# A decoder block on one core: the first norm's squares taken from transposed blocks, the first unit's weight remainders by accumulating transfers, and the rotation tables beside the gated units

## The chip, the core and the metric

The kernel runs on 1 core of one Trainium2 chip. The time is device microseconds of one execution of the whole block, and what counts is the median of several runs. Three runs of the kernel before took 1307.81, 1310.59 and 1313.95 us.

## The reference

One layer of a decoder, 512 tokens of width 1024, all in float32. In order: half a gated feed-forward network (hidden width 2816), a mixer with two branches (a convolution over 31 tokens with a layer norm, and a dilated attention with rotary position codes), a second half network, a gated embedding of the layer, and a last norm.

```python
h = h + 0.5 * swiglu(rms_norm(h, g_ffn1), w_ffn1_gate, w_ffn1_up, w_ffn1_down)
u = rms_norm(h, g_mix)
z = u @ w_in                              # conv gates | q | k | v | merge gates
y_conv = conformer_conv(a_glu, ...)       # glu, 31 taps, layer norm, silu, @ w_conv_out
q, k = rotary(q, cos, sin), rotary(k, cos, sin)
y_attn = o.reshape(b, s, ATTN_OUT_W) @ w_attn_out
h = h + (g_a * y_conv + g_b * y_attn) @ w_mix_out
h = h + 0.5 * swiglu(rms_norm(h, g_ffn2), w_ffn2_gate, w_ffn2_up, w_ffn2_down)
h = h + sigmoid(rms_norm(h, g_ple) @ w_ple_gate) * (p @ w_ple_proj)
return rms_norm(h, g_final)
```

Here `swiglu(x)` is `(silu(x @ w_gate) * (x @ w_up)) @ w_down`, and `cos` and `sin` come from the tokens' positions.

## The kernel before, in words

**Precision.** TensorE multiplies in a shortened float32. So each operand is split into a high part `h` (ScalarE copies it to the short type) and a remainder `l`, and a product is three matmuls: high by high, high by low, low by high (`mm3`, L458). A weight tile of 128 x 1024 is a *slab*. Its remainder is made in one of two ways. In `split_one` (L392) ScalarE makes `h` and VectorE subtracts, `l = r - h`. In `early_one` and `remainder` (L369 to L390) ScalarE writes `-h` into `l`, and a transfer issued by POOL adds the raw slab `r` to it in memory; ScalarE copies twice and VectorE does nothing. `by_dma` (L256) says which slabs go the second way. Raw slabs `wr`, sums `s`, `wh` and `wl` share sixteen buffers.

**The order.** `slab_order` (L132) lists all slabs, and `slab` (L440) loads, sums and splits ahead of use by fixed counts. There is no scheduler: each engine gets its instructions in the order in which the code is run, and waits in order.

**A network** (`ffn`, L779). Gate and up columns come in eleven units. Unit 0 is computed plainly: `plain` runs over the eight 128-row pieces of the input in two halves, four slabs (`gq`), into banks `pg` and `pu`. Units 1 to 10 (`gate_up`, L901) and the down steps (`down`, L953, called `dn` 1 to 5) use seven products in place of eight: B11, B21, T2, T1, T3, B22, T4, on sums of input quarters (`forms`, `form_pair`) and of weight quarters (`sum_one`). A product of a unit is 24 matmuls, with its result in banks `pa`, `pe` or `pd`. Unit 0's result goes through a plain down step (`down_plain`, L975) late in the network, where it needs its own split `hidh`, `hidl` (`keep`, L784, L790 and L792). `PLAN` (L73) is the order: units 1, 2, 3, `dn` 1, and so on to units 8, 9, `dn` 4, unit 10, the plain step, `dn` 5.

**The norm's factor.** The input is used unnormalised, and the factor of each token, 1/rms, is multiplied in after the matmuls. `token` (L871) computes it: sums of squares, a root by VectorE (`rsqrt`, L558), and two diagonal matrices. `on_all` (L618) spreads it over all partitions by two matmuls into a tile `R`. `gated` (L816) then makes unit 0's result from `R` and the four banks `pg` and `pu`; `others` makes the parts for T3 and T4. In the first network the squares are eight ScalarE passes over the columns of `x` with seven VectorE additions, and eight small matmuls (`ss`, L593) in the middle of the second half. The block's rows are made by `row_block` (L1088): four transposes of `x` by TensorE into a bank `tp` and a ScalarE copy; eight of these, from a list `turns`, one behind each of the first eight products.

**The tables** (`tables`, L1036) are some 36 VectorE instructions on 128 x 512 and two sines on ScalarE, put into a queue `bg` when unit 2 of the first network begins. `background(n)` runs the next `n` entries of `bg`; the counts `TABLES`, `TABLES_P` and `TABLES_D` place them beside products of the first network.

**The convolution.** For each pair of channel tiles of the gated units (`glu`, L1159; c = 0 to 7), `conv_start` puts some 64 entries into `bg`, which VectorE works off beside the gated units, the attention and the merge gates: six beside each half of a gated unit from c = 1, and six beside each merge gate. When `bg` is empty, `half` and `side` (L1525 to L1534) run the steps of the layer norm, `lns`: mean, centring, root, spreading to `R`, eight products with `R` (L1496), eight Silus (L1500) and splits into `cvh`, `cvl` (L476, L477). What is left of them by the end of the attention projection (banks `pb`) is run there at once, ahead of the eight `co` units (banks `py`), which need all eight `cvh` and `cvl`.

Of the kernel before, what the change touches and what calls it, by code (L numbers as in the profile page):

```python
# [18 lines left out]
P = 128  # L19
S = 512  # L20
D = 1024
# [27 lines left out]
N_NORM = {"1": ((1, 2), (1, 7)), "2": ((0, 6), (1, 3))}  # L49
# [30 lines left out]
TABLES = {"T3": 1, "B22": 1}  # L80
TABLES_P = 1
TABLES_D = {"B21": 1, "T3": 1, "B22": 1}
# [71 lines left out]
def block_kernel(ctx: ExitStack, tc: tile.TileContext, a, out):  # L154
# [101 lines left out]
    def by_dma(key):  # L256
        return product(key) in BY_DMA or key[0] in POOLED + RAISED or key[0] == "gq" and key[2] > 0
# [254 lines left out]
    def begin(norm):  # L512
# [40 lines left out]
        for c in range(KD):  # L553
            norm.add(x[c])
# [11 lines left out]
    class Norm:  # L566
# [18 lines left out]
        def total(self, m, by=None):  # L585
# [5 lines left out]
            for b in range(NB):  # L591
                for i, t in enumerate(every):
                    PE.matmul(p[:, b:b + 1], by_class(t)[:, b] if by else t[:, b * P:(b + 1) * P], mean[:, 0:1], start=i == 0,  # L593
                              stop=i == len(every) - 1)
            V.tensor_scalar(m, p[:, :NB], EPS, None, op0=OP.add)

        def by_token(self, diag=True, *by):
            m, y, t = (small.tile([P, NB], F32, name=name(q), tag="nt" + q, bufs=2) for q in "myt")
            self.total(m, *by)
# [11 lines left out]
        def spread(self):  # L611
            p = bank("R")
# [5 lines left out]
        def on_all(self):  # L618
            p, R = self.spread(), T("R")
# [4 lines left out]
    class Rows(Norm):  # L624
# [6 lines left out]
        def add(self, b, x_):  # L631
            A.activation(T("sq"), h[b][:, x_ * S:(x_ + 1) * S], AF.Square, scale=D ** -0.5,
# [146 lines left out]
    def ffn(n, xs, u, norm, out_, soon_=None, last_=None):  # L779
# [45 lines left out]
        def forms():  # L825
# [24 lines left out]
            for c, t12 in enumerate(t12s):  # L850
# [4 lines left out]
                flush(2)  # L855

# [14 lines left out]
        def token():  # L871
            y = norm.by_token(True, *([True] if n == "1" else []))
# [28 lines left out]
        def gate_up(j):  # L901

            ps = {q: bank(q) for q in ("pa", "pe", "pd")}
            t = {}
# [5 lines left out]
            for q in PRODUCTS:  # L910
                wh, wl = slab((n, ("gu", j), q))
                p = ps[BANKS[q]]
                while any(q not in z for z in xn):
                    next_job()
                quarters_of(p, q, wh, wl, [z[q] for z in xn])
                if q in ("B11", "T2", "T1"):
# [30 lines left out]
                background(TABLES.get(q, 0))  # L947
                if turns:
                    turns.pop(0)()
# [834 lines left out]
```

## Time and profile before

| what | value |
|---|---|
| profiled execution, its own time | 1308.47 us |
| its span | 1306.7 us |
| TensorE busy | 1272.3 us, 97% |
| VectorE busy | 1070.6 us, 82% |
| ScalarE busy | 756.1 us, 58% |
| POOL busy (it issues transfers) | 219.9 us, 17% |
| transfers by POOL, share of the 16 DMA engines | 51.2% |
| transfers by SP and ScalarE, share | 20.8% |

In the profile PE is TensorE, DVE is VectorE, ACT is ScalarE, and L736 is line 736 of the kernel. A line of instructions gives start and duration in us, then line, operation, and output and input by the program's names, then the count; in brackets stands how long the engine had been idle before it, and what ended that. Matmuls overlap, so the time that one takes from its neighbours is the distance of two starts, not its duration. In a table by stretch each engine has its busy time and, in brackets, its instructions; behind POOL's stands the clock that TensorE was granted, as a share of full speed. A line of waits gives the total in us, how often, and the longest.

### The profile page before, as it was taken

How to read it: one execution, taken by the hardware profiler on the slowest of the kernel's cores; microseconds unless marked ns; L12 is line 12 of the kernel's file. 1: busy time of each engine (PE TensorE's matmuls, PEld its weight loads, DVE VectorE, ACT ScalarE, POOL GpSimd, SP SyncE). 2: the span in 40 equal slices, each digit the busy share in tenths (PEclk: the TensorE clock that was granted, in tenths of full speed). 3: DMA queues.
4: the chain of work that ended last, by engine and by line, in shares of the span. 5: the costliest groups of instructions: out<-in, count | busy, mean ns of one | idle time of the engine just before them, and what ended most of it. 6: DMA issues, size and time to landing. Idle time of an engine off the chain costs nothing.

```text
span 1306.7 us, 20040 instructions
## 1 busy us (share of the span) xinstructions
PE 1272.3 (97%) x7546; PEld 1128.7 (86%) x7546; DVE 1070.6 (82%) x1733; ACT 756.1 (58%) x1098; POOL 219.9 (17%) x284
## 2 busy tenths in 40 slices
PE   8799999999999999999999999999999999999997
PEld 7799989897788889898988888888898999998786
DVE  8679898989767987777788866698988888887975
ACT  7576656665653235656475545355676766665573
POOL 0011111111132223323232222100111111111000
PEclk9899999999899999999999999999999999999999
DMA  7367776867798889888787877755568687777531
GB/s 248 89 164 187 194 178 165 208 139 179 167 217 185 194 187 178 161 193 153 166 163 179 193 173 180 197 129 162 145 178 210 148 208 169 192 201 179 147 97 65
DMA packets 120265, 224.43 MB, mean 172 GB/s; under 512 B 19048, under 2 KB 63464, under 8 KB 120168
## 3 DMA queue, kind: packets, MB, share of 16 engines
q0 software_dynamic: 44416, 136.33, 51.2%
q1 hardware_dynamic: 75464, 86.56, 20.8%
q8 instruction: 59, 0.97, 0.3%
q14 instruction: 38, 0.31, 0.1%
q10 hardware_dynamic: 288, 0.26, 0.1%
HBM read 164.36 MB, written 2.13 MB: 127 GB/s over the span
## 4 chain that ended last, share of the span: by engine, by line
PE 78%; DVE 8%; DMA 5%; issue 3%; ACT 2%; DVEq 0%; SPq 0%; POOL 0%; POOLq 0%; ACTq 0%
PE pa L736 4%; PE pa L737 4%; PE pa L739 4%; PE pq L459 4%; PE pq L460 4%; PE pq L461 4%; PE pa L746 3%; DMA wl<-wr 3%; PE pg L459 3%; PE pa L747 3%; PE pg L461 3%; PE pa L751 3%; PE pg L460 3%; DMA wr<-in_w_ffn_down 2%; PE pd L739 2%
## 5 line engine op out<-in xcount | busy, mean ns | idle before, releaser
L374 POOL DMA_DIRECT2D wl<-wr x104 | 89.2, 858 | 671.5 <-ACT wl L372 515.6
L403 DVE TENSOR_TENSOR wl<-s,wh 128x1024 fp32r<-128x1024 f32 x96 | 117.3, 1222 | 56.2 <-ACT wh L402 55.6
L1136 DVE SCALAR_TENSOR_TENSOR acc<-glu,taps,acc 128x511 f32<-128x511 f32 (+14 forms) x240 | 161.6, 733 | 0.0
L737 PE MATMUL pa<-bl,wh 128*128 128x256 f32 x480 | 120.3, 287 | 8.0 <-DVE bl L834 7.9
L736 PE MATMUL pa<-bh,wh 128*128 128x256 f32 x480 | 120.0, 287 | 3.7 <-ACT p L918 3.7
L372 ACT ACTIVATE wl<-wr 128x1024 fp32r<-128x1024 f32 x104 | 109.0, 1048 | 18.1 <-PE pd L751 8.3
L402 ACT ACTIVATE wh<-s 128x1024 fp32r<-128x1024 f32 x96 | 100.5, 1051 | 28.0 <-PE pa L751 7.9
L386 ACT ACTIVATE wh<-wr 128x1024 fp32r<-128x1024 f32 x104 | 108.8, 1046 | 1.9 <-PE pd L751 1.0
L372 ACT ACTIVATE wl<-wh 128x1024 fp32r<-128x1024 f32 x76 | 79.4, 1050 | 51.3 <-DMA wh<-in_w_in 32.4
L737 PEld LDWEIGHTS pa<-bl,wh 128*128 128x128 f32 x480 | 93.5, 195 | 9.0 <-DVE bl L834 9.0
L736 PEld LDWEIGHTS pa<-bh,wh 128*128 128x128 f32 x480 | 93.5, 195 | 4.5 <-ACT p L918 4.5
L459 PE MATMUL pq<-xsh,wh 128*128 128x512 f32 x224 | 88.7, 396 | 0.0
L460 PE MATMUL pq<-xsl,wh 128*128 128x512 f32 x224 | 87.3, 390 | 0.0
L461 PE MATMUL pq<-xsh,wl 128*128 128x512 f32 x224 | 87.3, 390 | 0.0
L374 POOL DMA_DIRECT2D wl<-in_w_in x56 | 48.6, 868 | 220.9 <-ACT wl L372 210.2
L739 PE MATMUL pa<-bh,wl 128*128 128x256 f32 x480 | 68.2, 285 | 0.0
L459 PE MATMUL pg<-xsh,wh 128*128 128x512 f32 x160 | 64.0, 400 | 0.3 <-DVE xsh L487 0.3
L460 PE MATMUL pg<-xsl,wh 128*128 128x512 f32 x160 | 63.2, 395 | 0.7 <-DVE xsl L488 0.6
L461 PE MATMUL pg<-xsh,wl 128*128 128x512 f32 x160 | 62.9, 393 | 0.0
L739 PEld LDWEIGHTS pa<-bh,wl 128*128 128x128 f32 x480 | 62.7, 194 | 0.0
L762 DVE SCALAR_TENSOR_TENSOR gx<-pa,half,gx 128x512 f32<-128x512 f32 x80 | 56.3, 747 | 1.6 <-PE pa L751 1.6
L746 PE MATMUL pa<-wh,bh 128*128 128x512 f32 x136 | 53.9, 396 | 2.7 <-DVE gx L762 2.7
(352 smaller groups left out, 3802.4 us busy)
## 6 DMA issues: line engine op xcount, KB each, us to landing
wl<-wr POOLq DMA_DIRECT2D x104, 512.0 KB, 5.1
wh<-in_w_in POOLq DMA_DIRECT2D x56, 512.0 KB, 7.2
wl<-in_w_in POOLq DMA_DIRECT2D x56, 512.0 KB, 6.2
wr<-in_w_ffn_up SPq DMA_DIRECT2D x88, 256.0 KB, 4.9
wr<-in_w_ffn_down SPq DMA_DIRECT2D x44, 512.0 KB, 5.3
wr<-in_w_ffn_gate SPq DMA_DIRECT2D x86, 256.0 KB, 5.0
wh<-in_w_v POOLq DMA_DIRECT2D x16, 256.0 KB, 7.1
wl<-in_w_v POOLq DMA_DIRECT2D x16, 256.0 KB, 5.6
```

The lines of the kernel that those rows point to most:

```text
L372: A.activation(l.bitcast(F32R), h, AF.Copy, scale=-1.0)
L374: G.dma_start(to, src, accum_op=OP.add)
L386: A.activation(h, r, AF.Copy)
L402: A.activation(h, r, AF.Copy)
L403: V.tensor_sub(l, r, h.bitcast(F32))
L459: PE.matmul(ps, wh, xh, start=start, stop=False, skip_group_check=part)
L460: PE.matmul(ps, wh, xl, start=False, stop=False, skip_group_check=part)
L461: PE.matmul(ps, wl, xh, start=False, stop=stop, skip_group_check=part)
L736: PE.matmul(o, h[:, c], th, start=q in ("B11", "B21", "T1") and i == 0, stop=False, skip_group_check=True)
L737: PE.matmul(o, h[:, c], tl, start=False, stop=False, skip_group_check=True)
L739: PE.matmul(o, l[:, c], th, start=False, stop=i >= len(at) - 2, skip_group_check=True)
L1136: bg.append(lambda acc=acc, g=g, w=w, s=s: V.scalar_tensor_tensor(acc[:, s:], g[:, :S - s], w, acc[:, s:], op0=OP.mult, op1=OP.add))
```

## The change

Five things are changed together.

- *Squares.* The first network's sums of squares come from `row_block`: while a transposed block lies in its bank, ScalarE squares it with a sum along each row, and then copies it. All eight blocks now stand in the second half of unit 0, one at each k. `token` follows product B11 of unit 1, and `on_all`, `gated` and `others` follow B21.
- *Remainders.* The four products of unit 1 that VectorE split (T2, T1, T3, B22), in both networks, and the four `gq` slabs of the second network get their remainders by accumulating transfers.
- *Tables.* They are put into `bg` after the first network, ahead of the convolution's entries: ten run after the gated unit c = 0, the rest in the next free places.
- *Plain down step.* `hidh` and `hidl` are made from unit 9 on, a unit earlier, in both networks.
- *Smaller.* The banks of a unit are taken when first used, and in the second network `gated` comes ahead of `others`.

```diff
--- before.py
+++ after.py
...
-N_NORM = {"1": ((1, 2), (1, 7)), "2": ((0, 6), (1, 3))}
+N_NORM = ((0, 6), (1, 3))
...
-TABLES = {"T3": 1, "B22": 1}
-TABLES_P = 1
-TABLES_D = {"B21": 1, "T3": 1, "B22": 1}
...
-        return product(key) in BY_DMA or key[0] in POOLED + RAISED or key[0] == "gq" and key[2] > 0
+        return (product(key) in BY_DMA or key[0] in POOLED + RAISED or key[:2] == ("gq", "2")
+                or key[0] in ("1", "2") and key[1] == ("gu", EARLY))
...
-        for c in range(KD):
-            norm.add(x[c])
...
+        def spread(self, tag="ps"):
+            p = bank("R", tag)
...
+        def on_all(self, tag="ps"):
+            p, R = self.spread(tag), T("R")
...
+        def add(self, b, x_, src=None):
+            A.activation(T("sq"), h[b][:, x_ * S:(x_ + 1) * S] if src is None else src, AF.Square, scale=D ** -0.5,
                          accum_out=self.cols[:, x_ * NB + b:x_ * NB + b + 1])
 
...
                 flush(2)
+            flush(0)
...
             us_ = [lambda i=i: slab(("gq", n, 0, 2 * half + i)) for i in range(2)]
-            fs = {k: f for (at, k), f in zip(N_NORM[n], (token, lambda: R.append(norm.on_all()))) if at == half}
-            if soon_ and half == 0:
-                fs[2] = soon_
+            fs = {}
+            if n == "1" and half:
+                fs = {k: turns.pop(0) for k in range(KD)}
+            elif n == "2":
+                fs = {k: f for (at, k), f in zip(N_NORM, (token, lambda: R.append(norm.on_all()))) if at == half}
+                if half == 0:
+                    fs[2] = soon_
             done.append(plain(us_, fs))
             if half == (n == "1"):
                 others = forms()
             if n == "2":
                 work(10.9)
+        hooks = {}
         if n == "1":
+            while jobs:
+                next_job()
+
+            def spread(done=done, others=others):
+                R.append(norm.on_all("cv"))
+                gated(*done)
+                while jobs:
+                    next_job()
+                others()
+                done.clear()
+            hooks = {"B11": token, "B21": spread}
+        else:
             gated(*done)
             others()
             work(10.9)
-        else:
-            others()
-            gated(*done)
-            work(10.9)
         done = others = None
 
...
-            ps = {q: bank(q) for q in ("pa", "pe", "pd")}
-            t = {}
+            ps, t = {}, {}
...
+                if BANKS[q] not in ps:
+                    ps[BANKS[q]] = bank(BANKS[q])
                 p = ps[BANKS[q]]
                 while any(q not in z for z in xn):
                     next_job()
                 quarters_of(p, q, wh, wl, [z[q] for z in xn])
+                if q in hooks:
+                    hooks.pop(q)()
...
-                background(TABLES.get(q, 0))
-                if turns:
-                    turns.pop(0)()
...
-                if not last:
-                    background(TABLES_D.get(q, 0))
...
-                    background(2 * TABLES_P)
...
-                if key[1] == KF // 2 - 1:
+                if key[1] == KF // 2 - 2:
                     keep(0, early[0])
                     early[0] = None
-                if n == "1" and key[1] == 2:
-                    tables()
...
-    norm = Norm()
-    x, xs, u1 = begin(norm)
-    norm.flush()
+    norm = Rows()
+    x, xs, u1 = begin()
...
     def row_block(b, j):
 
         p = bank("tp", "cv")
         for i in range(KD // 2):
             PE.transpose(p[:, i * P:(i + 1) * P], by_class(x[4 * j + i])[:, b], ident)
+        norm.add(b, j, p)
         A.activation(h[b][:, j * S:(j + 1) * S], p, AF.Copy)
...
-    background(len(bg))
+    tables()
...
-        if c == 1:
+        if c == 0:
+            background(10)
             rc, rs = tabs["cos"], tabs["sin"]
-            V.tensor_mul(rc, rc, R[0])
-            V.tensor_mul(rs, rs, R[0])
+            for t in (rc, rs):
+                bg.append(lambda t=t: V.tensor_mul(t, t, R[0]))
         if c % 2:
             conv_start((c - 1, c), glus)
             glus = []
```

On TensorE, in the first network, these rows stood in the second half of unit 0, between its next to last and its last k:

```order
L460 MATMUL pu_295<-xsl_192,wh_259 128x512
L461 MATMUL pu_295<-xsh_191,wl_260 128x512
L613 MATMUL R_382<-diag_339,one_r 128x512
L614 MATMUL R_382<-diag_340,one_r 128x512
L459 MATMUL pg_294<-xsh_197,wh_259 128x512
L460 MATMUL pg_294<-xsl_198,wh_259 128x512
```

The matmuls of `R` stand now in unit 1, behind the last matmuls of B21 (`pe`) and ahead of the first of T2 (`pa`):

```order
L735 MATMUL pe_520<-xsh_192,wl_284 128x256 x2
L735 MATMUL pe_520<-xsh_198,wl_284 128x256 x2
L609 MATMUL R_545<-diag_493,one_r 128x512
L610 MATMUL R_545<-diag_494,one_r 128x512
L732 MATMUL pa_449<-bh_403,wh_347 128x256
L733 MATMUL pa_449<-bl_404,wh_347 128x256
```

They moved from before B11 to behind B21, so T2 stands behind the factor of the norm.

On VectorE, between the attention projection (`pb`) and the first `co` unit (`py`), the eight products with the layer norm's `R` and the remainders `cvl` lay spread among the products with `pb`:

```order
L1496 TENSOR_TENSOR cv_5729<-cv_5729,R_7875 128x512
L1565 TENSOR_TENSOR sg_7237<-sg_7237,pb_7901 128x512
L1496 TENSOR_TENSOR cv_6960<-cv_6960,R_7875 128x512
L1496 TENSOR_TENSOR cv_6974<-cv_6974,R_7875 128x512
L477 TENSOR_TENSOR cvl_7919<-cv_4666,cvh_7918 128x512
L477 TENSOR_TENSOR cvl_7924<-cv_4668,cvh_7923 128x512
L1565 TENSOR_TENSOR sg_7282<-sg_7282,pb_7932 128x512
```

Now all of them come behind the last of those:

```order
L1571 TENSOR_TENSOR sg_7407<-sg_7407,pb_7953 128x512
L1502 TENSOR_TENSOR cv_4728<-cv_4728,R_7967 128x512
L1502 TENSOR_TENSOR cv_4775<-cv_4775,R_7967 128x512
L1502 TENSOR_TENSOR cv_5920<-cv_5920,R_7967 128x512
L1502 TENSOR_TENSOR cv_5922<-cv_5922,R_7967 128x512
L1502 TENSOR_TENSOR cv_7105<-cv_7105,R_7967 128x512
L1502 TENSOR_TENSOR cv_7140<-cv_7140,R_7967 128x512
L475 TENSOR_TENSOR cvl_7978<-cv_4728,cvh_7977 128x512
```

On TensorE the two matmuls that make this `R` moved with them, from behind the projection's second product to behind its eighth, straight ahead of `py`.

On VectorE again, the remainders `hidl` for the plain down step stood in unit 10 of the first network, behind the first of the sums `s` for `dn` 5:

```order
L340 TENSOR_TENSOR s_593_3649<-wr_3577,wr_3579 128x1024
L931 TENSOR_TENSOR p_3563<-p_3563,pd_3456 128x512
L936 TENSOR_TENSOR p_3563<-p_3563,R_385 128x512
L792 TENSOR_TENSOR hidl_3451<-tu_407,hidh_3450 128x512
L792 TENSOR_TENSOR hidl_3453<-tu_408,hidh_3452 128x512
L1045 SCALAR_TENSOR_TENSOR ang_747<-n_748,ang_747 128x512
L344 TENSOR_TENSOR s_596_3687<-s_593_3649,wr_3581 128x1024
```

They stand now at the end of unit 9, ahead of the results `u` of that unit and of the first updates of `gx` by `dn` 4:

```order
L944 TENSOR_TENSOR p_3116<-p_3116,pd_3127 128x512
L949 TENSOR_TENSOR p_3116<-p_3116,R_548 128x512
L788 TENSOR_TENSOR hidl_3001<-tu_552,hidh_3000 128x512
L788 TENSOR_TENSOR hidl_3003<-tu_553,hidh_3002 128x512
L351 TENSOR_TENSOR s_524_3229<-wr_3055,s_521_3164 128x1024
L954 TENSOR_TENSOR u_3004<-p_3152,p_3116 128x2x256
L936 TENSOR_TENSOR u_3004<-pa_3015,p_3040 128x2x256
L401 TENSOR_TENSOR wl_3269<-s_521_3164,wh_3268 128x1024
L758 SCALAR_TENSOR_TENSOR gx<-pa_3262,half_503,gx 128x512
```

They moved past the sums of `dn` 5, to the front of `dn` 4.

More of the change, by code (lines that the diff above doesn't have):

```diff
@@ L510, in gain, with begin @@
         return gains[:, v + c:v + c + 1]
-    def begin(norm):
+    def begin():
         rs_ = [W("wr") for _ in range(2)]
@@ L583, in flush, with total @@
                 self.last = None
-        def total(self, m, by=None):
+        def total(self, m):
             every = [self.acc]
@@ L592, in total, with by_token @@
                 for i, t in enumerate(every):
-                    PE.matmul(p[:, b:b + 1], by_class(t)[:, b] if by else t[:, b * P:(b + 1) * P], mean[:, 0:1], start=i == 0,
+                    PE.matmul(p[:, b:b + 1], t[:, b * P:(b + 1) * P], mean[:, 0:1], start=i == 0,
                               stop=i == len(every) - 1)
             V.tensor_scalar(m, p[:, :NB], EPS, None, op0=OP.add)
-        def by_token(self, diag=True, *by):
+        def by_token(self, diag=True):
             m, y, t = (small.tile([P, NB], F32, name=name(q), tag="nt" + q, bufs=2) for q in "myt")
-            self.total(m, *by)
+            self.total(m)
             rsqrt(m, y, t)
@@ L609, in by_token @@
             return y
-        def spread(self):
-            p = bank("R")
+        def spread(self, tag="ps"):
+            p = bank("R", tag)
             PE.matmul(p, one_r, self.diag[0], start=True, stop=False)
@@ L616, in spread @@
             return p
-        def on_all(self):
-            p, R = self.spread(), T("R")
+        def on_all(self, tag="ps"):
+            p, R = self.spread(tag), T("R")
             A.activation(R, p, AF.Copy)
@@ L871, in token @@
         def token():
-            y = norm.by_token(True, *([True] if n == "1" else []))
+            y = norm.by_token()
             t = tiny("half", NB)
```

2 lines of the change are left out of this document (removed).

## The prediction

> **What bounds the kernel now.** I read the page first, then who waited for whom on TensorE, then TensorE's instructions in order of time, then busy time and granted clock by stretch.
>
> ```profile
> span 1306.7 us, 20040 instructions
> ...
> PE 1272.3 (97%) x7546; PEld 1128.7 (86%) x7546; DVE 1070.6 (82%) x1733; ACT 756.1 (58%) x1098; POOL 219.9 (17%) x284
> ```
> ```profile
> PE pa L737 <- DVE bl L834: 7.9, 2, 4.8
> PE pd L986 <- DVE hidl L792: 3.8, 3, 2.4
> ```
>
> TensorE is the bound: 97% busy, 34.4 us without work. Only what fills one of its gaps, makes one, or halves its clock moves the end. The largest sum is 7.9 us in the first unit; here is that stretch (start, duration, in brackets the idle time before and who ended it).
>
> ```profile
> 19.03 0.39 PE L459 MATMUL pg<-xsh,wh 128*128 128x512 f32 x1
> 20.39 0.39 PE L459 MATMUL pg<-xsh,wh 128*128 128x512 f32 x1
> ...
> 23.34 2.03 PE L593 MATMUL ss<-mean,sq 128*128 128x1 f32 x8 [1.43 <-DVE sq L582]
> 25.23 0.50 PE L459 MATMUL pg<-xsh,wh 128*128 128x512 f32 x1
> ...
> 35.60 0.28 PE L736 MATMUL pa<-xsh,wh 128*128 128x256 f32 x1
> 38.47 0.65 PE L1092 MATMUL tp<-ident,x 128*128 128x128 f32 x4
> 38.87 0.36 PE L736 MATMUL pe<-xsh,wh 128*128 128x256 f32 x1
> ...
> 48.29 0.58 PE L737 MATMUL pa<-bl,wh 128*128 128x256 f32 x1 [4.76 <-DVE bl L834]
> 59.68 0.58 PE L737 MATMUL pa<-bl,wh 128*128 128x256 f32 x1 [3.14 <-DVE bl L834]
> 74.78 0.36 PE L736 MATMUL pe<-xsh,wh 128*128 128x256 f32 x1
> ```
>
> One k of the second half takes 1.36 us (19.03 to 20.39), one product of a unit 2.87 (35.60 to 38.47), the four transposes of a block 0.40 (38.47 to 38.87). From 35.60 to 74.78 stand eight products and eight blocks, 22.96 + 3.20 = 26.2 us of work in 39.2: 13.0 are lost, 7.9 by waiting and the rest by the clock (PEclk, the column ahead of the DMA share):
>
> ```profile
> 25.50:29.00 3.50, 3.50 (x10) 2.68 (x10) 3.03 (x14) 0.00 (x0) 0.16 (x1) 0.51 1.04 195
> 46.00:49.40 3.40, 1.11 (x4) 0.93 (x4) 3.40 (x7) 1.09 (x2) 0.00 (x0) 0.50 0.63 137
> 70.00:75.00 5.00, 5.00 (x44) 5.00 (x43) 2.15 (x4) 3.35 (x6) 0.00 (x0) 1.00 0.86 220
> 339.60:343.00 3.40, 3.03 (x6) 2.01 (x7) 2.22 (x4) 1.49 (x3) 0.00 (x0) 0.50 0.93 282
> 343.00:346.40 3.40, 3.40 (x9) 2.63 (x9) 3.40 (x5) 2.95 (x5) 0.86 (x1) 0.50 0.45 92
> 930.00:933.50 3.50, 2.59 (x21) 2.59 (x22) 3.25 (x4) 3.50 (x5) 0.46 (x1) 1.00 0.34 124
> ```
>
> After a wait the clock is halved for one or two stretches of 3.4 us, each costing up to 1.7 us more; not after every one (930). [...]
>
> **The first unit.** Durations on the other engines:
>
> ```profile
> 34.90 1.66 ACT L831 ACTIVATE bh<-t 128x512 fp32r<-128x512 f32 x3
> ```
> ```profile
> 24.34 1.22 DVE L340 TENSOR_TENSOR s<-wr,wr 128x1024 f32<-128x1024 f32 x1
> 26.79 0.16 DVE L595 TENSOR_SCALAR m<-ss 128x4 f32<-128x4 f32 x1
> 31.02 0.17 DVE L874 TENSOR_SCALAR half<-y 128x4 f32<-128x4 f32 x1
> ```
> ```profile
> L372 ACT ACTIVATE wl<-wr 128x1024 fp32r<-128x1024 f32 x104 | 109.0, 1048 | 18.1 <-PE pd L751 8.3
> ...
> wl<-wr POOLq DMA_DIRECT2D x104, 512.0 KB, 5.1
> ```
>
> Removed: eight squares, seven adds, the 1.43 us wait, the eight small matmuls (23.34 to 25.23) and the half clock behind them. The second half now holds all eight blocks: 19.03 + 8 × (1.36 + 0.40) = 33.1. A block's bank is free only after ScalarE has squared and copied it (about 1.1 us, by the 0.55 of a 512-wide copy, 1.66 / 3), between weight copies of 1.05; the two banks will run out once, about 1.3 us, an estimate. The unit starts at 34.4 instead of 35.60.
>
> Added: the matmul of R now stands between B21 and T2. B21 ends at 34.4 + 5.74 = 40.1. The last block is transposed at about 33; its square and copy (1.1), four `bh` copies (2.2), and on VectorE, which follows them in turn, the last subtractions and one 1.22 us sum put the root's start between 39 and 40, and root to diagonals takes 4.2 (26.79 to 31.02): R at about 44, a wait of some 4 us that holds T2 and all behind it on TensorE; on VectorE the products of `gated` are queued behind it. T3 waits as before, since its parts come after `gated`. And the second sum of the next unit, ahead of those parts on VectorE, takes the buffer of a raw slab that an accumulating transfer reads until it lands (5.1 us median behind an 1.05 us copy): VectorE gives up subtractions, but waits for transfers instead. So two waits again. I take their loss with the clock as the 13.0 of before: 34.4 + 22.96 + 0.46 for R + 13.0 = 70.8, against 74.78, and allow 0.5 for more queueing: **−3.5 us**. Without any wait it would be 34.4 + 23.4 = 57.8 (−17); with 4 us more waiting +0.5. The nearest rows are the two waits that stand there, so I hold −7 to +0.5 for the range.
>
> **Tables out of the first network.**
>
> ```profile
> L1045 DVE SCALAR_TENSOR_TENSOR ang<-n,ang x6: 685/686/689, 192.3 to 341.1; 128x512 f32<-128x512 f32 x6
> ```
>
> Some 36 VectorE instructions of at most 0.69 leave a stretch whose TensorE waits are mostly for transfers and ScalarE: −0.5 (0 to −2). Where they go now, VectorE's share is its 82% at most, and the load of the positions moves on SP's queue behind the last `down` slabs, far ahead of its first user; ScalarE's two more table loads fall on an engine 58% busy. Cost +0.3 (0 to 1, an instruction or two late). But ten run after unit 0, at most twelve in unit 1's free places, and about fifteen push the convolution's queue back: two to three gate units, since those take six each. That is the next part.
>
> **The layer norm after the convolution.** Its steps begin when that queue is empty. The order shows the result: R, which stood after the second of the eight products of the attention projection, now stands after the last, straight ahead of the `co` units, with all eight normalisations, Silus and splits behind it. Before:
>
> ```profile
> 797.69 0.40 PE L614 MATMUL R<-diag,one_r 128*128 128x512 f32 x1
> 814.27 0.39 PE L459 MATMUL py<-cvh,wh 128*128 128x512 f32 x1
> ```
> ```profile
> 801.48 2.48 DVE L1496 TENSOR_TENSOR cv<-cv,R 128x512 f32<-128x512 f32 x4
> 819.91 0.69 DVE L1578 TENSOR_TENSOR sg<-sg,py 128x512 f32<-128x512 f32 x1 [3.43 <-PE py L461]
> ```
> ```profile
> 807.27 0.80 ACT L1500 ACTIVATE cv<-cv,gx 128x512 f32<-128x512 f32 x1
> 808.10 0.63 ACT L476 ACTIVATE cvh<-cv 128x512 fp32r<-128x512 f32 x1
> 808.64 0.80 ACT L1500 ACTIVATE cv<-cv,gx 128x512 f32<-128x512 f32 x1
> ```
>
> Some 16.6 us lay between R and its first user; none of TensorE's work is left there. From R's start: 0.23 + 0.40 until R is whole, 0.7 for the first product with it, 0.80 + 0.63 to the first `cvh`: 2.8. Seven more pairs at 1.37 (807.27 to 808.64): 12.4. The last `cvl` (0.69) and two matmuls: 13.5. R's 0.46 and the unit's own 5.6 (814.27 to 819.91) were paid before: **+7.5 us**. Lower bound: six normalisations (0.6 each) precede the first `cvl`, 4.9; upper bound: two halved windows, 11.
>
> **The plain down step and what was moved.** The waits there, and in the second network:
>
> ```profile
> 339.97 0.79 PE L986 MATMUL pd<-wh,hidl 128*128 128x512 f32 x1 [2.43 <-DVE hidl L792]
> ```
> ```profile
> 336.76 1.22 DVE L340 TENSOR_TENSOR s<-wr,wr 128x1024 f32<-128x1024 f32 x1 [3.21 <-DMA wr<-in_w_ffn_down]
> ```
> ```profile
> 302.48 0.48 PE L746 MATMUL pa<-wh,bh 128*128 128x512 f32 x1 [0.65 <-DVE gx L762]
> ```
> ```profile
> 930.91 0.39 PE L736 MATMUL pa<-bh,wh 128*128 128x256 f32 x1 [2.51 <-ACT p L918]
> ```
> ```profile
> 1206.19 0.50 PE L986 MATMUL pd<-wh,hidl 128*128 128x512 f32 x1 [1.18 <-DVE hidl L792]
> 1225.16 0.47 PE L746 MATMUL pa<-wh,bh 128*128 128x512 f32 x1 [1.72 <-DVE gx L762]
> ```
>
> `hidl` stood behind a sum that waits for a transfer (336.76); it now comes a unit earlier: 2.43 and the two halved stretches (3.2) go, −5.6. Two subtractions of 0.69 stand ahead of the T2 of `dn` 4, whose wait of 0.65 grows by up to 1.4 (+1.2); and the sum still waits for its transfer, so TensorE reaches `dn` 5 earlier than its parts: +1.5 (0 to 3.4). Sum **−2.9**.
>
> **Second network.** Unit 1's four more slabs move four VectorE subtractions to four ScalarE copies (1.05 each) exactly where TensorE waits 2.51 for ScalarE: +1.2 (0 to 3; a gain down to −2 if VectorE was late too), and a halved window half of the time, 0.8. The `gq` slabs come by POOL, 17% busy, ahead of their use as the others do: 0 (to 2.5, half a transfer late). `gated` now stands ahead of the T3 and T4 parts there, four products of 0.69 in front of what T3 needs 5.7 us later: 0 (to 2). `dn` 4 again +1.2; the 1.18 at the plain step goes; the 1.72 at `dn` 5 stays. Sum **+2.0** (−2 to +5).
>
> Sum: −3.5 − 0.5 + 0.3 + 7.5 − 2.9 + 2.0 = +2.9. The profiled execution took 1308.47 us, so 1311.4; the median of the runs, 1310.59, is 2.1 above it, which would make 1313.5. I forecast **1312**, between the two: no change, as 0.5% (6.6 us) is about what a measurement of this kernel can tell from none.
>
> **Rivals.** (1) The new waits halve the clock. At `co` TensorE is under half busy for 13 us; two windows there cost 3.4, one window each at T2 of the second network, both `dn` 4 and both `dn` 5 up to 1.7: 2.9 + 3.4 + 5 × 1.7 − 0.8 (counted above) = +14, about 1322. It decides where a wait leaves under half of a 3.4 us stretch busy: 2.43 did (339.60), 2.51 did not (930.00). (2) VectorE was what was late at both first units: with four 1.22 us subtractions fewer, T3's wait goes (3.14 and a halved window, 4.8), the second network comes out at −2 instead of +2.0, and `dn` 5 gives nothing back (1.5): 2.9 − 4.8 − 4.0 − 1.5 = −7.4, about 1301. For it: both waits of before are for VectorE's `bl`; against: the transfer that its buffer now waits for, and a second network that waits for ScalarE. [...]
>
> **Chances.** No change 0.70; (1) 0.16; (2) 0.10; (3) 0.04. So faster 0.10, same 0.70, slower 0.20. The range takes in the bounds of the first unit and of `co` and part of (1): 1304 to 1320.
>
> **What would show it.** Right: a gap before R of 3 to 4 us near 40; one before T3 near 53; none at `pd` `hidl`; the first `py` unit over 12 us long, paced by ScalarE. Wrong: a `py` unit under 7 us, a unit 1 without gaps, or `hidl` still waited for.

## The result, and the profile after

The changed kernel took 1317.2 us in the median of 18 runs, the kernel before 1311.12 in as many beside them: a ratio of 1.0046, with a 95% interval of 1.0035 to 1.0058. That is 6 us slower, just under the 0.5% that was named as the bound of no change. One run of the changed kernel took 1791.33 us, and the profiled run of a kernel below (dma_net1) 2537.78, far above the other runs of the same kernel; the ratios leave such runs out, and dma_net1 has no stages below. The profiled execution took 1317.04 us, against 1308.47 before: 8.6 us more, since the profile of before lies 2.7 us under its median and that of after 0.2.

The head of the page:

```profile
span 1315.2 us, 20075 instructions
...
PE 1273.8 (97%) x7538; PEld 1127.4 (86%) x7538; DVE 1054.0 (80%) x1714; ACT 765.8 (58%) x1116; POOL 238.9 (18%) x308
```

VectorE lost 16.6 us of work and ScalarE gained 9.7; TensorE is as full as before. Whom it waited for (total, times, longest):

```profile
PE pa L742 <- DVE gx L758: 8.1, 4, 2.1
PE pa L732 <- ACT bh L827: 6.0, 1, 6.0
PE pa L732 <- ACT p L931: 4.3, 1, 4.3
PE R L609 <- DVE diag L604: 2.6, 1, 2.6
PE py L457 <- ACT cvh L474: 2.4, 1, 2.4
PE py L458 <- DVE cvl L475: 2.2, 4, 1.6
```

Against the waits of before, that for `hidl` is gone, of the 2.9 for transfers (`wl<-wr`) 0.3 is left, and of the 7.9 for `bl` 0.7; the lines shown are new or longer waits. Where the time went is read from the starts of the same matmuls in both kernels. Of before, the first product with `pb` (the first gated unit) and the first of the second network:

```profile
375.47 0.48 PE L459 MATMUL pb<-xsh,wh 128*128 128x512 f32 x1
898.34 0.48 PE L459 MATMUL pg<-xsh,wh 128*128 128x512 f32 x1
```

Of after, the same, with the other places on which the prediction rested:

```profile
35.90 0.28 PE L732 MATMUL pa<-xsh,wh 128*128 128x256 f32 x1
44.44 0.47 PE L609 MATMUL R<-diag,one_r 128*128 128x512 f32 x1 [2.63 <-DVE diag L604]
58.92 0.58 PE L732 MATMUL pa<-bh,wh 128*128 128x256 f32 x1 [6.02 <-ACT bh L827]
74.74 0.28 PE L732 MATMUL pe<-xsh,wh 128*128 128x256 f32 x1
369.93 0.48 PE L457 MATMUL pb<-xsh,wh 128*128 128x512 f32 x1
811.98 0.50 PE L457 MATMUL py<-cvh,wh 128*128 128x512 f32 x1 [2.41 <-ACT cvh L474]
814.07 0.78 PE L458 MATMUL py<-cvl,wh 128*128 128x512 f32 x1 [1.58 <-DVE cvl L475]
901.53 0.48 PE L457 MATMUL pg<-xsh,wh 128*128 128x512 f32 x1
936.26 0.39 PE L732 MATMUL pa<-bh,wh 128*128 128x256 f32 x1 [4.30 <-ACT p L931]
1179.17 0.61 PE L742 MATMUL pa<-wh,bh 128*128 128x512 f32 x1 [1.96 <-DVE gx L758]
```

So three stages, and the same split of every kernel of this study (first network: to the first `pb`; middle: from there to the first `pg` of the second network; second: from there to the end of the last matmul; the kernels are explained below):

| kernel | first network | middle | second | ratio to before, 95% interval |
|---|---|---|---|---|
| before | 375.5 | 522.9 | 399.5 | 1 |
| after | 369.9 | 531.6 | 405.3 | 1.0046 (1.0035 to 1.0058) |
| gate8 | 370.9 | 525.9 | 405.0 | 1.0012 (0.9994 to 1.0029) |
| tables_back | 379.5 | 523.2 | 401.9 | 1.0080 (1.0059 to 1.0100) |
| dma_net1 | - | - | - | 1.0033 (1.0020 to 1.0045) |
| keep_only | 378.8 | 522.9 | 403.9 | 1.0040 (1.0027 to 1.0054) |
| glu7 | 369.2 | 523.9 | 406.4 | 1.0029 (1.0013 to 1.0045) |
| glu7_keep8 | 368.8 | 524.7 | 403.4 | 0.9988 (0.9974 to 1.0001) |
| glu7_oldkeep | 371.6 | 523.9 | 402.0 | 0.9972 (0.9956 to 0.9987) |
| glu7_dma1 | 370.3 | 523.9 | 400.2 | 0.9972 (0.9960 to 0.9985) |
| tables_only | 368.5 | 524.0 | 400.2 | 0.9945 (0.9929 to 0.9961) |
| best | 369.2 | 524.0 | 395.9 | 0.9908 (0.9894 to 0.9922) |
| nodma | 365.5 | 524.6 | 397.5 | 0.9910 (0.9895 to 0.9925) |
| tables_gated | 370.2 | 524.0 | 400.8 | 0.9924 (0.9903 to 0.9946) |

From before to after: -5.5, +8.7 and +5.8, together +9.0, and 0.5 less behind the last matmul. One trace stands behind each row, so small differences in a column are not to be read: even the start of unit 1 lies between 34.75 and 35.90 in after, glu7 and best, whose code is the same up to there. Nor is the profiled run always a typical one: it took 3.9 us less than the median in tables_back and 2.2 less in nodma, and 4.1, 3.9 and 4.6 more in keep_only, glu7_oldkeep and tables_gated. The last column was measured on several chips, on which the median of before lay between 1306.8 and 1312.7; kernels of one group below ran on one chip and are compared best with one another. The granted clock in the second half of unit 0, and behind three of the waits (in each row the length of the stretch, then the busy time and instructions of the engines, and behind POOL's the granted clock):

```profile
19.00:36.00 17.00, 15.55 (x82) 12.82 (x81) 5.82 (x9) 14.66 (x31) 2.70 (x3) 1.00 0.59 129
814.00:817.50 3.50, 3.44 (x8) 2.72 (x9) 3.08 (x7) 3.40 (x7) 0.00 (x0) 0.52 0.00 0
937.00:940.40 3.40, 3.40 (x19) 3.40 (x18) 1.55 (x2) 3.00 (x4) 1.71 (x2) 0.50 1.01 192
1179.30:1182.70 3.40, 3.40 (x9) 2.56 (x10) 2.83 (x4) 1.59 (x2) 0.84 (x1) 0.51 1.04 283
```

The first row: with all eight blocks transposed between the products, the last four at one block of 0.39 in each 1.87 us, the clock stayed at 1.00. The other three rows are the first rival, in three of its places: behind the `py` wait, behind T2 of the second network and behind its `dn` 4.

### The profile page after: what moved, and what is told of

The parts are those of the page before. It is cut to its first block, busy times and chain, and to the rows that moved or that the text cites. A ratio compares the mean times of both kernels' runs of the same rounds, so it can differ in the third digit from the quotient of the medians.

```text
span 1315.2 us, 20075 instructions
## 1 busy us (share of the span) xinstructions
PE 1273.8 (97%) x7538; PEld 1127.4 (86%) x7538; DVE 1054.0 (80%) x1714; ACT 765.8 (58%) x1116; POOL 238.9 (18%) x308
## 5 line engine op out<-in xcount | busy, mean ns | idle before, releaser
L401 DVE TENSOR_TENSOR wl<-s,wh 128x1024 fp32r<-128x1024 f32 x90 | 109.8, 1220 | 55.0 <-ACT wh L400 55.0
L370 ACT ACTIVATE wl<-wh 128x1024 fp32r<-128x1024 f32 x80 | 83.7, 1051 | 57.6 <-DMA wh<-in_w_in 29.5
L400 ACT ACTIVATE wh<-s 128x1024 fp32r<-128x1024 f32 x90 | 94.1, 1049 | 35.8 <-DMA wl<-wr 13.1
```

The lines of the kernel that those rows point to most:

```text
L370: A.activation(l.bitcast(F32R), h, AF.Copy, scale=-1.0)
L400: A.activation(h, r, AF.Copy)
L401: V.tensor_sub(l, r, h.bitcast(F32))
```

## The experiments

The theory with which they began: the place of the layer norm costs 8.7 us in the middle; the accumulating transfers of unit 1 cost in the second network, since ScalarE must copy twice; the earlier `hidl` only moves a wait; and the tables' leaving won what was won. The rival: the waits come from something else that stands in the same place (ScalarE's pace at `co`, the new order of `gated` and `others`, the transfers), and undoing these parts one by one changes nothing.

### First group: one part each

**gate8**: the changed kernel, and

```diff
-N_GATE = 6
+N_GATE = 8
```

> The changed kernel with one number changed: eight entries of the background queue beside each merge gate in place of six, so that the queue is empty as early as in the kernel before and the layer norm's R stands again behind the second product of the attention projection. Theory (the tables' fifteen or so entries push the layer norm out of its cover, which costs 8.5 us between the projection and the end of the co units): the waits at py go, and the time falls from 1317.2 to about 1309, at most 2 us higher if VectorE is late beside the gates. Rival (the co units start late for another reason, such as ScalarE being slower there): it stays at 1315 to 1318.

The ratio was 1.0012 in place of 1.0046, where the theory gave 0.998 to 1.000. The waits at `py` are gone, and the middle fell from 531.6 to 525.9. Of the 3.0 us that remain over the kernel before, 1.3 are three waits at the attention's last step, which did not wait there; the first is

```profile
738.55 0.39 PE L457 MATMUL po<-pt,vh 128*128 128x256 f32 x1 [0.60 <-ACT pt L1373]
```

So the layer norm's place is the cause of the loss in the middle, and its rival (ScalarE's pace) is out. Eight entries in a row beside a merge gate seem to be too many there; glu7, below, spreads them and has no such wait.

**tables_back**: the changed kernel with the tables in the first network again, by the counts of before:

```diff
+                background(TABLES.get(q, 0))
...
+                    background(TABLES_D.get(q, 0))
...
+                    background(2 * TABLES_P)
...
+                if n == "1" and key[1] == 2:
+                    tables()
```

> The changed kernel with the rotation tables back in the first network, as the kernel before has them; all else as changed. Theory: the same 8.5 us at co are won, and what the first network won between unit 2 and dn 4 (up to 4.1 us) is lost, if that came from the tables: 1309 to 1313, and the first product with pb starts near 373. Rival for that gain (it came from the squares, the remainders or the later start of bank use, not from the tables): pb starts near 370 still and the time is 1309.

It was slower than the changed kernel: 1.0080. The middle is as before (523.2), but the first network takes 379.5, 9.6 us longer than in the changed kernel. Both forecasts had this too small. Part of it is the earlier `hidl`, which does not go with tables in the first network: keep_only, below, has both and stands at 378.8. The largest waits of tables_back from 60 to 380 us:

```profile
PE pe L750 <- DMA wl<-wr: 4.3, 4, 1.4
PE pa L745 <- DVE gx L761: 2.8, 2, 2.3
```

**dma_net1**: the changed kernel, and

```diff
-                or key[0] in ("1", "2") and key[1] == ("gu", EARLY))
+                or key[0] == "1" and key[1] == ("gu", EARLY))
```

> The changed kernel with unit 1's four remainders by accumulating transfer in the first network only; in the second VectorE subtracts them again. Theory (the four further ScalarE copies are what made T2 of the second network wait 4.30 in place of 2.51 and halved the clock there): the wait is back at about 2.5 with a full clock, 3.5 us fewer, 1313.7. Rival (the wait grew because gated stands ahead of others there, or by the four gq slabs): it stays at 4 or more, and the time at 1316 to 1318.

1.0033, against 1.0046: in the direction expected, but the intervals overlap, and there are no stages to compare. It was repeated on another base, below.

**keep_only**: the kernel before, and

```diff
-                if key[1] == KF // 2 - 1:
+                if key[1] == KF // 2 - 2:
                     keep(0, early[0])
```

> The kernel before with hidh and hidl a unit earlier in both networks, nothing else. Theory: in the first network 5.7 fewer at the plain down step, 1.2 more at dn 4, 2.0 more at dn 5; in the second 2.2 fewer, 3.1 more (with a halved window) and 1.1 more: together about 0, 1310 to 1311. Rival (the waits at dn 4 and dn 5 of the changed kernel come from its transfers or its missing tables, not from the two subtractions): only the gains stay, about 1304.

1.0040: this part alone makes the kernel before 5 us slower, against a forecast of none. The wait for `hidl` goes, but `dn` 4 pays at once, with a halved stretch behind it, and `dn` 5 waits too (the granted clock over the run is 0.987, before 0.990); the second network, with little to win at the plain step, loses 4.4. Up to 1.7 of that is a halved stretch behind T2, though its wait, 2.50, is that of before, and the profiled run was the second slowest of twelve, so 5 us is the better figure. `dn` 4 of the first network:

```profile
305.76 0.47 PE L746 MATMUL pa<-wh,bh 128*128 128x512 f32 x1 [2.07 <-DVE gx L762]
```

The way there, in the changed kernel on VectorE, with one line of ScalarE:

```profile
292.54 0.69 DVE L788 TENSOR_TENSOR hidl<-tu,hidh 128x512 fp32r<-128x512 f32 x1 [0.62 <-ACT hidh L786]
293.15 1.22 DVE L351 TENSOR_TENSOR s<-wr,s 128x1024 f32<-128x1024 f32 x1
...
295.61 0.42 ACT L675 ACTIVATE b<-u 128x256 fp32r<-128x256 f32 x1 [3.10 <-DVE u L936]
...
297.53 1.23 DVE L401 TENSOR_TENSOR wl<-s,wh 128x1024 fp32r<-128x1024 f32 x1 [1.96 <-ACT wh L400]
298.67 1.40 DVE L758 SCALAR_TENSOR_TENSOR gx<-pa,half,gx 128x512 f32<-128x512 f32 x2
```

The update `gx` empties the bank that T2 of `dn` 4 needs. It stands behind a split that waits for ScalarE's `wh`, and ScalarE comes to it only when it has the results `u`, which stand behind the subtractions. So two subtractions of 0.6 us at the front reach TensorE through both engines; T2 waited 0.65 before and 1.96 after.

### Second group: the layer norm in its place, then one part undone at a time

**glu7**: the changed kernel with the entries made good earlier:

```diff
-N_GLU = (0, 0) + (6,) * 14
+N_GLU = (0, 0) + (7,) * 14
```

> The changed kernel with seven background entries beside each half of a gated unit in place of six; all else as changed. The fourteen more entries make good what the tables pushed back, so the layer norm's R stands again behind the second product of the attention projection. Theory (place, not amount, of the tables' work costs the 8.3 us at co, and the 2.6 us that eight entries beside the merge gates cost in the attention's last step are not due here): ratio to the kernel before about 0.998, 1308.5 on the scale where the changed kernel has 1317.2. Rival (VectorE becomes late beside the gated units instead): 1.001 or more, with waits of TensorE between 380 and 460.

The middle is 523.9, 7.7 less than after, and in it TensorE has one wait above 0.2 us, of 1.3: the place was the cost, not the amount. The profiled execution took 1309.66 us. The ratio, 1.0029, fell less than the forecast 0.998, and its interval overlaps that of after; the two were not run on one chip.

**glu7_keep8** and **glu7_oldkeep**: as glu7, with `keep` at unit 8 or back at unit 10:

```diff
-                if key[1] == KF // 2 - 2:
+                if key[1] == KF // 2 - 3:
```

```diff
-                if key[1] == KF // 2 - 2:
+                if key[1] == KF // 2 - 1:
```

> As the run with seven entries, and hidh and hidl made from unit 8 on in place of unit 9, in both networks, so that their subtractions stand beside units 8 and 9, no longer straight ahead of dn 4. Theory (these two subtractions and the copies ahead of them are what T2 of dn 4 waits for, 1.96 with a halved stretch after it, in both networks): these waits fall to 0.7 or less and the time by 3 to 6 us against the run with seven entries. Rival (the wait at dn 4 is for ScalarE's weight copies, whatever stands ahead): no difference.

> As the run with seven entries, but hidh and hidl from unit 10 on as in the kernel before. Theory (moving them alone made the kernel before 5 us slower, so undoing it should win): dn 4 loses its wait (2 to 3 us in each network), dn 5 too, and the plain step gets its wait for hidl back (2.4 and two halved stretches, 5.7 us, in the first network; 1.2 and one in the second): between -2 and +2 us against the run with seven entries. Rival (with the tables gone VectorE is on time for hidl even there): the wait stays away and 4 to 6 us are won.

Both won: 0.9988 and 0.9972, against 1.0029 on the same chip. At unit 8 the wait of `dn` 4 fell from 1.96 to 1.02 in both networks and no stretch was halved there (the granted clock over the run is 0.992, in glu7 0.988). At unit 10 it is gone, and the wait for `hidl` did not come back: in the first network the longest of that kind is 0.2. That is what the rival had forecast. In a kernel that has the rest of the change, nothing had to be moved. The tables' leaving alone does not bring this about, though the rival gave it as the reason: in tables_only, below, `hidl` is late at its old place.

**glu7_dma1**: as glu7, with the edit of dma_net1.

> As the run with seven entries, and unit 1's four remainders by accumulating transfer in the first network only. Theory: T2 of the second network's unit 1 waits 2.5 in place of 4.3, without a halved stretch behind it: 3.5 us fewer than the run with seven entries. Rival (the wait is for what the order of gated and others puts there): no difference.

0.9972, in the medians 5.3 us faster than glu7, where 3.5 were expected. T2 of unit 1, in the second network, in glu7:

```profile
927.08 0.58 PE L732 MATMUL pa<-bh,wh 128*128 128x256 f32 x1 [3.97 <-ACT p L931]
```

and in glu7_dma1:

```profile
925.25 0.39 PE L732 MATMUL pa<-bh,wh 128*128 128x256 f32 x1 [0.95 <-ACT p L931]
```

The two halved stretches behind it went with it; the granted clock over the run rose from 0.988 to 0.992. The reason stands on ScalarE in the changed kernel:

```profile
931.85 1.04 ACT L370 ACTIVATE wl<-s 128x1024 fp32r<-128x1024 f32 x1
...
934.69 1.04 ACT L384 ACTIVATE wh<-wr 128x1024 fp32r<-128x1024 f32 x1
935.64 0.57 ACT L931 ACTIVATE p<-pa 128x512 f32<-128x512 f32 x1
```

The copy `p` empties the bank `pa` that T2 needs. It takes 0.57 us and stands behind four weight copies (`wl`, `wh`, `wl`, `wh`), two of which are there only because the remainders go by transfer. In glu7_dma1 one is left ahead of it:

```profile
923.67 1.04 ACT L400 ACTIVATE wh<-s 128x1024 fp32r<-128x1024 f32 x1
924.62 0.58 ACT L931 ACTIVATE p<-pa 128x512 f32<-128x512 f32 x1
```

Three copies fewer, at a distance of 0.95, are 2.85 of the 3.02 us that T2's wait lost.

### Third group: parts alone, and the best of them together

**tables_only**: the kernel before with the tables beside the gated units and seven entries; nothing else of the change.

```diff
-N_GLU = (0, 0) + (6,) * 14
+N_GLU = (0, 0) + (7,) * 14
...
-                background(TABLES.get(q, 0))
...
-    background(len(bg))
+    tables()
...
-        if c == 1:
+        if c == 0:
+            background(10)
```

> The kernel before with one part of the change alone, the tables beside the gated units, and seven background entries in place of six so that the layer norm keeps its place. Theory (VectorE's table work was what made the first network's transfers, dn 5 and the plain step late): 5 to 9 us won there, among them the wait of 2.43 for hidl, and at most 1 us lost beside the gated units: ratio 0.994 to 0.997. Rival (what the first network won came from the other parts): 0.999 to 1.002, with the wait for hidl still there.

0.9945, 7 us faster than before, all of it in the first network (368.5). Its waits from 60 to 380 us are one line. Before had six in that stretch; the largest, 3.1 for `bl` at 59.68, is in tables_only too, at 59.34, and of the other five the second fence shows the one for transfers:

```profile
PE pd L983 <- DVE hidl L792: 3.8, 2, 3.6
```

```profile
PE pe L751 <- DMA wl<-wr: 2.9, 3, 1.2
```

The page of before put these 2.9 us down to transfers, and they went when VectorE was relieved. One of them, in the kernel before, followed back through VectorE, ScalarE and POOL:

```profile
149.29 0.69 DVE L1045 SCALAR_TENSOR_TENSOR ang<-nl,ang 128x512 f32<-128x512 f32 x1
...
152.36 0.68 DVE L1045 SCALAR_TENSOR_TENSOR ang<-nh,ang 128x512 f32<-128x512 f32 x1
...
154.69 0.69 DVE L923 TENSOR_TENSOR u<-pa,p 128x512 f32<-128x512 f32 x1
...
155.41 0.42 ACT L679 ACTIVATE b<-u 128x256 fp32r<-128x256 f32 x1 [2.31 <-DVE u L923]
...
169.30 1.05 ACT L372 ACTIVATE wl<-wr 128x1024 fp32r<-128x1024 f32 x1
170.64 0.86 POOL L374 DMA_DIRECT2D wl<-wr  x1 [1.04 <-ACT wl L372]
177.91 1.20 PE L751 MATMUL pe<-wl,bh 128*128 128x512 f32 x4 [0.85 <-DMA wl<-wr]
```

Two table instructions stand ahead of the result `u`, for which ScalarE waits; ScalarE's copy, POOL's issue and the transfer follow, and the transfer that TensorE waits for is the last link of that chain. Without the two, in tables_only, the same `u`, `b`, copy and issue come 1.55 us earlier, 0.34 of which were there already ahead of the first (the issue is at 169.09), TensorE's product there only 1.00 earlier; the transfer, which took 7.2 us from issue to landing and now 5.6, is there in time, and the wait is gone.

The wait for `hidl` stayed, against the expectation (3.6 us). It starts with a VectorE sum that waits for its slab, here 5.00 us:

```profile
331.43 1.22 DVE L340 TENSOR_TENSOR s<-wr,wr 128x1024 f32<-128x1024 f32 x1 [5.00 <-DMA wr<-in_w_ffn_down]
```

In the run best, with the same order at that place, the slab was there 2.9 us earlier:

```profile
328.58 1.23 DVE L338 TENSOR_TENSOR s<-wr,wr 128x1024 f32<-128x1024 f32 x1 [1.36 <-DMA wr<-in_w_ffn_down]
```

Why it landed earlier there is open; the loads on SP's queue just behind it are the same, and from 324 us on the DMA engines are busy for 0.92 of the time or more in both.

**best**: the changed kernel with the edits of glu7, glu7_oldkeep and dma_net1.

> The changed kernel with seven entries, hidh and hidl from unit 10 on as before, and unit 1's remainders by accumulating transfer in the first network only. Theory (the two undone parts act in different places, dn 4 and unit 1 of the second network, so their gains add: each gave 0.0057): ratio 0.991 to 0.993. Rival (what is won early is lost at the next wait): 0.996 or more.

0.9908, with an interval of 0.9894 to 0.9922: 12 us faster than before. The forecast, which added the two gains, holds. T2 in the second network waits 0.70, and no stretch is halved between 355.5 us and the end of the products (granted clock 0.992 over the run).

**nodma**: as best, without accumulating transfers for unit 1 in either network:

```diff
-        return (product(key) in BY_DMA or key[0] in POOLED + RAISED or key[:2] == ("gq", "2")
-                or key[0] in ("1", "2") and key[1] == ("gu", EARLY))
+        return (product(key) in BY_DMA or key[0] in POOLED + RAISED or key[:2] == ("gq", "2"))
```

> As the run best, and unit 1's remainders subtracted by VectorE in the first network too, so that no accumulating transfer is behind unit 1. Theory (T3 of the first network waits 6 us because VectorE's second sum waits 3 us for an accumulating transfer that still reads its buffer): that wait goes, four subtractions of 1.22 come on VectorE instead, and unit 2 starts 0 to 3 us earlier. Rival (the subtractions hold up VectorE as they did in the kernel before): the wait before T3 or T2 is as long or longer, 0 to 3 us more than best.

Inside unit 1 the theory held in its direction: the wait shrank, but did not go. In the changed kernel VectorE's second sum had waited for an accumulating transfer, and the parts for T3 are queued behind it:

```profile
52.10 1.22 DVE L338 TENSOR_TENSOR s<-wr,wr 128x1024 f32<-128x1024 f32 x1
56.31 1.22 DVE L342 TENSOR_TENSOR s<-s,wr 128x1024 f32<-128x1024 f32 x1 [3.00 <-DMA wl<-wr]
```

Without the transfers T3 waits 3.80, against 6.15 in best, while R's wait ahead of T2 is 3.76 in place of 2.63:

```profile
56.56 0.58 PE L731 MATMUL pa<-bh,wh 128*128 128x256 f32 x1 [3.80 <-ACT bh L826]
```

Unit 2 starts 2.8 us earlier (68.29, 71.12 in best). But the whole kernel measured 0.9910, the same as best, with intervals of 2 us either way; the gain of unit 1 does not show in the time.

**tables_gated**: tables_only, with the two calls of the second network exchanged:

```diff
-            others()
             gated(*done)
+            others()
```

> As the run tables_only (the kernel before with the tables beside the gated units and seven entries), and in the second network gated ahead of others, as the changed kernel has it. In the run best T2 of that network's unit 1 waits 0.70, in tables_only 2.53 with a halved stretch. Theory (the order does it: ScalarE's two Silus of gated no longer stand between the parts and the copy that empties bank pa): the wait falls below 1.2, the halved stretch goes, 2 to 4 us fewer, ratio 0.992 to 0.993. Rival (the four gq slabs by accumulating transfer do it, by relieving VectorE): no difference, 0.9945 and a wait of 2.5.

The theory fell: T2 still waits for the copy `p`, 2.39 us, though no halved stretch follows.

```profile
926.60 0.38 PE L736 MATMUL pa<-bh,wh 128*128 128x256 f32 x1 [2.39 <-ACT p L918]
```

The ratio, 0.9924, is the one that the theory gave, but its interval overlaps that of tables_only, and the second network took 400.8 against 400.2, with a wait of 3.7 for `hidl` in it. So what brings T2's wait from 2.5 to 0.70 in best is not the order of the two calls alone. The four `gq` slabs by transfer, and the forms that are finished (`flush(0)`) before `gated`, remain; they were not told apart.

## Why the prediction was right, and which of its terms were not

The forecast was no change, 1312 in a range of 1304 to 1320. The measured ratio lies in that bound, at its slow end, and the sum of the terms, +2.9, stands against 8.6 between the two profiles and 6 in the medians. The stages bear this out in part. The first network as a whole came near its forecast, -6.9 against -5.5, but by luck: its three terms were each off, and the errors cancelled for the most part. The middle was right, and the second network cost almost three times its term. Stage by stage:

- **First unit, forecast -3.5, measured 0.0** (unit 2's B21 at 74.74, before 74.78). The two waits came as named, R's 2.63 at 44.44 (about 4 were forecast) and T3's behind the sum that waits for a transfer. But the unit started at 35.90, not 34.4, for the most part since one k with its block took 1.87 us in place of 1.76, and the second wait was not 3.1 but 6.0 and 0.7. The term took the loss of before for the new one; nodma shows that the transfers lengthen T3's wait by 2.35 (6.15 less 3.80) and shorten R's by 1.1.
- **Tables out of the first network, forecast -0.5: the step that was furthest off.** By the starts of the same product, the last before `dn` 4's T2, the changed kernel had won 4.1 us there (300.63 became 296.54); put back they cost 9.6 (with the earlier `hidl`), moved alone they won 7. The step said that the waits of that stretch were "mostly for transfers and ScalarE" and so VectorE's relief was worth nothing. The last link of a chain was taken for its cause.
- **The layer norm, forecast +7.5 and +0.3 beside the gated units, measured +8.7** in the middle. R went where the order said, and one stretch was halved, inside the bounds given. The first `py` unit took 11.6 us from 811.98 to the next, 5.6 before and over 12 by the sign named, paced by ScalarE's pairs at 1.37. gate8 and glu7 show that it is the place.
- **Plain down step, forecast -2.9.** From `dn` 4 to the first `pb` the changed kernel won a further 1.4. The wait for `hidl` did go and `dn` 4 and `dn` 5 got theirs (1.96 and 2.08); keep_only shows that without the rest of the change this part loses, and glu7_oldkeep that with it the old place is better.
- **Second network, forecast +2.0, measured +5.8.** Each wait was named, none was large enough. T2 waited 4.30, 1.8 more, and its halved stretch, counted at half, came; `dn` 4 waited 1.96 with a halved stretch. By the starts of the same products T2 cost 3.7 in place of 2.0 and `dn` 4 3.0 in place of 1.2; `dn` 5, at nothing in the sum, cost 0.6, and the plain step won 1.7 in place of 1.2. This was the first rival in two of its places, 3.5 us more than the terms here, and up to 1.7 at `py`.

A gain was in the change: its tables' part alone, with the layer norm kept in its place, is worth 0.55%. Three things gave more than that back: the layer norm's place, the earlier `hidl`, and unit 1's transfers in the second network. The rest of the change (the squares, the `gq` slabs, the smaller parts) is in best, 5 us faster than tables_only; these parts were not run alone, so which of them won that is open.

## What to carry to other kernels

A wait that a profile puts down to a transfer, on a chain that another engine feeds, is not evidence that this engine has time to spare: follow the transfer's issue back before pricing relief at nothing. When work is moved into a queue that others share, count what it pushes back, to the last entry; here one number, six or seven entries, decided whether 16 us of cover stayed. And a copy of 0.6 us that empties a bank belongs ahead of weight copies of 1.05 in the same engine's order; where TensorE already waits for it, as at T2 here, three copies fewer, 2.85 us, took 3.02 off the wait.

## What was not expected of the hardware

Whether a wait halves the clock does not follow from its length alone. A wait of 1.96 at `dn` 4 was followed by a halved stretch in the second network (1179.30) and not in the first (299.56). T2's wait of 2.53 in tables_only was followed by one, its 2.39 in tables_gated was not. In the kernel before, the halved stretches at 46.02, 59.68 and 339.57 begin 6, 10 and 92 steps of 3.41 us behind the one at 25.55 (314.02 over 92 is 3.413); in the changed kernel those at 56.36, 814.12, 937.00 and 1179.35 begin 3, 225, 261 and 332 such steps behind the one at 46.12. The steps that hold the four waits, counted so from the halved stretches of each trace (the first two rows the first network's `dn` 4, the third the second network's, then T2 in tables_only and in tables_gated):

```profile
295.31:298.72 3.41, 2.29 (x11) 1.56 (x9) 1.45 (x3) 3.11 (x5) 0.00 (x0) 1.00 0.86 276
298.72:302.13 3.41, 2.56 (x11) 1.96 (x12) 3.41 (x6) 2.57 (x3) 0.85 (x1) 1.00 1.06 348
1175.94:1179.35 3.41, 1.45 (x7) 0.94 (x6) 2.21 (x3) 3.41 (x5) 0.07 (x1) 1.00 0.97 306
922.89:926.30 3.41, 1.20 (x10) 1.21 (x11) 3.06 (x5) 3.41 (x6) 0.00 (x0) 1.00 0.44 159
925.07:928.48 3.41, 1.89 (x15) 1.89 (x16) 3.41 (x5) 3.41 (x6) 0.00 (x0) 1.00 0.48 159
```

The first wait lies across two steps, in which TensorE was busy for 2.29 and 2.56 of 3.41; the third and the fourth row have it busy for 1.45 and 1.20, and the next step was halved; in the last it was busy for 1.89, and the next was not. The traces of before and after have 734 steps at full clock from 30 us on. The ten of them with TensorE busy for 1.45 us or less were each followed by a halved one, among them the one ahead of 339.57 in before, with 1.38. None of the other 724 was; the least busy of these have 1.48 (after, from 1230.55), 1.74 (before, from 926.66, with T2's wait of 2.51) and 1.79 (after, from 930.17). So here the same wait of 1.96 was followed by a halved stretch where it fell into one step, and by none where it lay across two, which bears out the first rival's "under half of a 3.4 us stretch" but for the step of 1.48, 0.43 of it. Ahead of 30 us one step is an exception: the one with the eight small matmuls `ss` in before, from 22.14, with 2.21 busy, was followed by a halved one too.
